# A hybrid encoder trunk in exact float32: FFN products in another order, two first weight blocks loaded together, small vectors through POOL's queue

## The chip, the cores and the metric

The kernel runs on one core of a Trainium2 chip. A core has five engines with queues of their own: TensorE (PE; its weight loads are listed as PEld), VectorE (DVE), ScalarE (ACT), GpSimd (POOL) and SyncE (SP), which here issues most of the DMA transfers. Each engine works its queue in order and waits on semaphores. The metric is device time in microseconds (us), the median of several runs.

## The reference

Two layers. Each projects x (512 x 1024) with one wide matrix, runs three mixers on the parts (retention with four heads, chunked attention with a relative bias, differential attention), gates and sums them, projects the sum, and applies a layer norm; then a SwiGLU feed-forward network (FFN) and a second norm.

```python
for l in range(DEPTH):
    h = jnp.einsum('bsd,de->bse', x, w_in[l])
    rq, rk, rv, rg, cq, ck, cv, dq, dk, dv, gates = jnp.split(h, splits, axis=-1)
    o_a = _retention(rq, rk, rv, rg, ret_norm_g[l])          # heads reshaped, left out here
    o_b = _chunk_attention(cq, ck, cv, ca_rel_bias[l])
    o_c = _diff_attention(dq, dk, dv, lam, lambda_init, da_norm_g[l])
    g = jax.nn.sigmoid(gates + b_merge[l]).reshape(B, S, N_BRANCHES, D)
    merged = sum over the branches of g[:, :, i] * (o_i @ w_branch_i[l])
    x = _layer_norm(DEEPNORM_ALPHA * x + merged @ w_out[l], ln1_g[l], ln1_b[l])
    u_gate, u_up = jnp.split(x @ w_ffn_in[l], 2, axis=-1)
    ffn = (jax.nn.silu(u_gate) * u_up) @ w_ffn_out[l]
    x = _layer_norm(DEEPNORM_ALPHA * x + ffn, ln2_g[l], ln2_b[l])
```

## The kernel before

**Numbers.** Every float32 operand is carried as a pair, hi and lo, in the type that TensorE takes at full rate. ACT casts hi, DVE subtracts to get lo (a "split"), and each product is three matmuls (`mm3`: hi by hi, hi by lo, lo by hi).

**Weights.** Weights come in blocks of up to 1 MB. A block is loaded by SP into one of four staging tiles (`st`), then split by ACT (`wh`) and DVE (`wl`) into one of three hi/lo buffer pairs. `Wt` does this in two halves (L151, L152), `Staged` in one piece (L260, L261).

**Seven products instead of eight.** Large products are done by a scheme of Strassen's kind on 2 x 2 blocks: seven products m1, m2, y, v, g, x, h, each of 24 matmuls of 512 columns, and sums of weights and activations beside them. In a `Chain` unit the weight sums are made in place, one after another, in a staging tile: the block is split for one product, then POOL issues an accumulating load (`more`, L179) that adds the next piece of weight from memory, and the result is the block of the next product of the chain: m1, then y, then x, then h. `ahead_c` makes the separate sum for g. In a `Close` unit DVE adds staged blocks (L234, L240). The activation sums are made by `Quarters.sums` (L293 to L296, then splits); the steps `s_q` (mixer) and `s_x1` (FFN) call it. `u_two` turns the seven results into outputs: x alone leads to 14 DVE operations (L740 to L746 and the callbacks); m1, g, v and y are copied out of PSUM by ACT (L734). In the FFN the callbacks are `gate_half` and `gated` (L1218), which multiply the two halves of a hidden tile (the `nat` tiles). `s_turn(pb, hf)` transposes two finished `nat` tiles on PE (L1230); `s_ready` and `s_twins` split the transposed tiles for the products of the output matrix.

**Order.** The program is a list of items, each with its weight blocks, a function and groups of side steps; weights are fetched until three blocks stand ready. Between the column tiles of an item (`between`), one group of side steps is placed; what is left follows the item.

```python
while at <= i or (at < len(items) and sum(map(len, ready)) < AHEAD):
    fetch()
pending.extend(groups)
fn(*ready.pop(0))
while pending:
    between()
```

The order of the items is written by hand. The order of the instructions on an engine's queue is then set by a scheduler, which by its own model of time lets a ready instruction pass one that waits; `keep_in_program_order` pins an instruction behind the one traced before it on its engine. So SP issues a load as soon as a staging tile is free by that model.

**The start.** The first item, `u_first`, needs three blocks: retention's q and k columns for two heads, and a gate. Block 0 is loaded in four pieces with two of the eight x tiles behind each (`load_x`), and split the same way (`split_x`, L589 and L590); the first two column tiles of block 0 run as the pieces arrive, blocks 1 and 2 follow. Retention's q and k go through `rotary` (two ACT copies, three DVE operations, then a split). After block 1 comes `vectors`: 7 loads of `rows`, a transpose on PE (`pcol`, L626), ACT's and DVE's copies of it, and 4 broadcast loads of `lv`; in layer 0 also `negate_bias`, a load, a negation and a store of the bias rows (`nrel`). All of these go through SP's queue.

**Retention.** `s_dh(h)` loads a decay tile (`dh`, 256 KB), `s_r1(h)` computes the scores (`psr`), multiplies by the decay (L795) and splits the result.

**FFN.** `u_ffn(i)` does 48 matmuls of 512 columns and its gate (`ffn_done`); `u_ffn_first` does the first two tiles by halves of the rows. `s_natural(t)` finishes the natural-layout rows of the norm (four DVE operations and two stores). Units p and q are the input products, o and w the output products; `fout_rest` does the remaining rows, and ends in `chase`, where each tile of rows is normalised behind its matmuls.

Of the kernel before, what the change touches and what calls it, by code (L numbers as in the profile page):

```python
# [17 lines left out]
P = 128  # L18
# [3 lines left out]
KT = D // P  # L22
# [4 lines left out]
DA_HEADS, DA_DH = 4, 64  # L27
# [29 lines left out]
def trunk(ctx, tc, x_in, xT_in, w_in, ret_norm_g, da_norm_g, lq1, lk1, lq2, lk2, w_a, w_b, w_c, b_merge, w_out,  # L57
# [22 lines left out]
    def f(ap):  # L80
        return ap.bitcast(F32)
# [44 lines left out]
    class Wt:  # L126


        def __init__(self, pieces, nk, beside=None):
            ncol = sum(ap.shape[1] for ap in pieces)  # L130
            n = nk * ncol
            st = wst.tile([P, 2048], F32, tag="st", name="st")[:, :n].rearrange("p (k c) -> p k c", k=nk)
            hi = wsp.tile([P, 2048], F32R, tag="wh", name="wh")[:, :n]
            lo = wsp.tile([P, 2048], F32R, tag="wl", name="wl")[:, :n]
            self.hi = hi.rearrange("p (k c) -> p k c", k=nk)
            self.lo = lo.rearrange("p (k c) -> p k c", k=nk)
            self.nk = nk
            h = max(nk // 2, 1) if beside is None else 2
            c0 = 0
            for ap in pieces:  # L140
                w = ap.shape[1]
                src = ap.rearrange("(k p) c -> p k c", p=P)
                for k in range(0, nk, nk if beside is None else h):
                    e = nk if beside is None else k + h
                    nc.sync.dma_start(st[:, k:e, c0:c0 + w], src[:, k:e])
                    if beside is not None:
                        beside[0](k, e)
                c0 += w
            for a in range(0, nk, h):
                b = min(a + h, nk)  # L150
                done = [nc.scalar.copy(self.hi[:, a:b], st[:, a:b]),  # L151
                        nc.vector.tensor_sub(self.lo[:, a:b], st[:, a:b], f(self.hi[:, a:b]))]  # L152
                if beside is not None:
                    for ins in done:
                        tc.keep_in_program_order(ins)
                    beside[1](a, b)

    class Halves:

# [395 lines left out]
    def run_items():  # L555
        ready, at = [], 0

        def fetch():
            nonlocal at
            specs, at = items[at][0], at + 1  # L560
            ready.append([])
            for sp in specs:
                first = at == 1 and not ready[-1]
                ready[-1].append(sp() if callable(sp) else Wt(*sp, beside=(load_x, split_x) if first else None))
# [12 lines left out]
        nc.tensor.transpose(warm[:, :P], ident, ident)  # L577


    def load_x(k0, k1):  # L580
        for k in range(k0, k1):
            xfs[0][k] = g(name="xf")
            nc.sync.dma_start(xfs[0][k], xT_in[P * k:P * k + P])

    def split_x(k0, k1):
        for k in range(k0, k1):
            xTs[0][k] = Pair("xT")
            src, pr = xfs[0][k], xTs[0][k]
            tc.keep_in_program_order(nc.scalar.copy(pr.hi, src))  # L589
            tc.keep_in_program_order(nc.vector.tensor_sub(pr.lo, src, f(pr.hi)))  # L590

    xTs = [[None] * KT for _ in range(DEPTH + 1)]
    xfs = [{} for _ in range(DEPTH + 1)]
# [2 lines left out]
    def layer(l):  # L596
# [8 lines left out]

        def negate_bias():
            t = small.tile([P, 96], F32, tag="nrel", name="nrel", bufs=1)
            nc.sync.dma_start(t, rel.rearrange("l h (r c) -> (l h r) c", c=96))
            nc.vector.tensor_scalar_mul(t, t, -1.0)
            nc.sync.dma_start(nrel, t)  # L610

        def vectors():
            if l == 0:
                negate_bias()

            rows = small.tile([64, P], F32, tag="rows", name="rows", bufs=1)
            nc.gpsimd.memset(rows, 0.0)
            r0 = 0
            for name, ap in (("bm", b_merge), ("rg", ret_norm_g), ("dg", da_norm_g), ("g1", ln1_g), ("b1", ln1_b),
                             ("g2", ln2_g), ("b2", ln2_b)):  # L620
                n = ap.shape[1] // P
                nc.sync.dma_start(rows[r0:r0 + n], ap[l:l + 1].rearrange("o (r c) -> (o r) c", c=P))
                v[name] = slice(r0, r0 + n)
                r0 += n
            psc = bank("pcol")
            nc.tensor.transpose(psc[:, :64], rows, ident[:64, :64])  # L626
# [49 lines left out]
        def u_first():  # L676
# [8 lines left out]

            def whole(*wts):
                ret_tables()
                banks = [bank("pt") for _ in range(2)]
                for k in range(KT):
                    for j in range(2):  # L690
                        a, c = xT[k], slice(P * j, P * j + P)
                        mm3(banks[j], wts[0].hi[:, k, c], wts[0].lo[:, k, c], a.hi, a.lo, k == 0, k == KT - 1)
                for i, w in enumerate(wts):
                    for j in range(2):
# [25 lines left out]
        def u_two(hv, acts, left_done, right_done):  # L720
# [16 lines left out]
            def x(j, ps):  # L737
                u, y, c = g(name="tu"), t["y", j], t.pop(("v", j))
                t["u", j] = u
                nc.vector.tensor_sub(u, ps, t.pop(("m1", j)))  # L740
                nc.vector.tensor_add(y, y, u)
                nc.vector.tensor_add(c, c, y)
                right_done(j, c)
                c = t.pop(("g", j))
                nc.vector.tensor_add(y, y, c)
                nc.vector.tensor_add(u, u, c)  # L746
                right_done(2 + j, t.pop(("y", j)))

            def m2(j, ps):
                c = g(name="tm")  # L750
# [5 lines left out]
                nc.vector.tensor_sub(u, ps, u)  # L756
                left_done(2 + j, u)

            use = {"x": x, "m2": m2, "h": h}
# [342 lines left out]

        w, p, q = u_two(Close(W, 0, 4, (CV, DV)), xq, v_away(cv, 64), v_away(dv, 128)), u_rvg(0), u_rvg(1)
        for (specs, fn), *groups in [
            (u_first(), [w["c"]]), (u_gate(0, 1), [w["a"], s_q(0)], [s_q(1)]), (w["m1"], [], [s_q(2)]), (u_gate(0, 2), [s_q(3)]),
            (w["g"],), (w["v"],), (w["m2"], [lam]), (w["y"], [p["c"]]), (w["x"],), (u_gate(0, 3),), (w["h"], [p["a"], s_dh(0)]),
            (p["m1"], [], [s_r1(0)]), (p["g"], [s_dh(1)]), (p["v"], [], [s_r1(1)]), (p["m2"],),
            (p["y"], [q["c"]]), (p["x"],), (u_rqk(rq, RQ, 1), [q["a"]]), (p["h"],),
            (q["m1"], [], [s_r2(0)]), (u_rqk(rk, RK, 1), [s_r2(1)], [s_r3(0)]), (q["g"], [], [s_r3(1)]),
            (q["v"], [s_dh(2)]), (q["m2"], [], [s_r1(2)]), (q["y"], [s_dh(3)]), (q["x"],), (u_cqk(0), [], [s_r1(3)]), (q["h"],),  # L1110
# [272 lines left out]

        p, q, o, w = u_fin(0), u_fin(1), fout_items(0), fout_items(1)
        for (specs, fn), *groups in [
            (u_ffn_first([8, 9]), [s_natural(0)], [s_x1(0)]),
            (p["m1"], [s_x1(1)], [p["c"], s_natural(1)]), (p["m2"], [s_x1(2)], [s_natural(2)]),
            (u_ffn(10), [s_x1(3), s_natural(3)]), (p["y"],), (p["v"],), (p["g"],), (p["x"],),
            (u_ffn(11), [], [s_turn(0, 0)]), (p["h"],), (q["m1"], [q["c"]], [s_turn(0, 1)]), (q["m2"],), (u_ffn(12),),
            (q["y"],), (q["v"],), (q["g"],), (q["x"],), (u_ffn(13), [], [s_turn(1, 0)]), (q["h"], [s_ready(0)], [s_ready(1)]),  # L1390
            (o["m1"], [], [s_turn(1, 1)]), (u_ffn(14), [s_twins(0)], [s_twins(1), o["c"]]), (o["m2"],), (o["y"],), (u_ffn(15),),
            (o["v"],), (o["x"],), (u_ffn(16),), (o["g"], [], [s_hid(0)]), (o["h"], [], [s_hid(1)]), (u_ffn(17), [s_hid(2)], [s_hid(3)]),
            (w["m1"],), (u_ffn(18), [], [w["c"]]), (w["m2"],), (w["y"],), (u_ffn(19),),
            (w["v"],), (w["x"],), (u_ffn(20),), (w["g"],), (w["h"],), (u_ffn(21),),
        ]:
            item(specs, fn, *groups)
        for it in fout_rest(0) + fout_rest(1):
# [60 lines left out]
```

## Time and profile before

| what | value |
|---|---|
| median of 3 runs | 1912.64 us (1911.21 to 1913.13) |
| the profiled execution, its own time | 1909.92 us |
| its span, first to last instruction | 1908.2 us |
| granted TensorE clock, mean | 0.997 |
| busy: PE, PEld | 1884.3 us, 1585.9 us |
| busy: DVE, ACT, POOL | 1354.5 us, 951.1 us, 101.6 us |
| DMA | 285.12 MB, 149 GB/s mean |

How to read the rows: a row of the timeline is the start in us, the duration, the engine, the line of the kernel, the operation, output tile <- input tiles, their shapes, and a count; in brackets the idle time of the engine just before, and what ended it. The table of waits gives, for an engine's line and what released it, the total, the number of times and the longest. PE's matmuls are pipelined: a row's duration is the time through the array, and the distance of two starts is the pace. "SPq" and "POOLq" are the issuing queues.

### The profile page before, as it was taken

To read this page: it belongs to the slowest core of one execution; us is meant where nothing else is said; L and a number is where in the kernel's file an instruction comes from. 1 tells how busy PE (TensorE), PEld (TensorE's weight loads), DVE (VectorE), ACT (ScalarE), POOL (GpSimd) and SP (SyncE) were. 2 spreads that over 40 slices of the span, in tenths; PEclk is the share of its full clock that TensorE was granted. 3 is DMA by queue.
4 is the path that set the end of the run, shared out by engine and by line. 5 is a ranking of instruction groups with operands and counts; after the bars stand their busy time and mean duration, and the time that the engine had idled before them with its cause. 6 is when DMAs were issued, how large, how long until landed. Compare 5 with 4: busy or idle time off the path is not lost. (4 is left out here: it accounts for less than half of the span.)

```text
span 1908.2 us, 24157 instructions
## 1 busy us (share of the span) xinstructions
PE 1884.3 (99%) x9170; PEld 1585.9 (83%) x9170; DVE 1354.5 (71%) x2157; ACT 951.1 (50%) x1581; POOL 101.6 (5%) x117
## 2 busy tenths in 40 slices
PE   9999999999999999999999999999999999999998
PEld 7888888888888878888898788888888888788886
DVE  5778866677666866886578788666775668677865
ACT  5545555566534544453255546555765344444530
POOL 0000000000001000000000000000000010010000
PEclk9999999999999999999999999999999999999999
DMA  8686343332254577664555844432322647785641
GB/s 258 189 258 164 121 163 106 118 122 67 70 193 124 165 188 188 166 159 129 153 170 175 253 131 144 165 106 94 122 78 72 215 89 189 173 215 151 157 130 44
DMA packets 240185, 285.12 MB, mean 149 GB/s; under 512 B 9550, under 2 KB 148932, under 8 KB 240068
## 3 DMA queue, kind: packets, MB, share of 16 engines
q1 hardware_dynamic: 216836, 237.43, 37.8%
q0 software_dynamic: 23232, 46.14, 13.9%
q8 instruction: 72, 1.18, 0.2%
q14 instruction: 45, 0.37, 0.1%
HBM read 260.42 MB, written 23.12 MB: 149 GB/s over the span
## 5 line engine op out<-in xcount | busy, mean ns | idle before, releaser
L122 PE MATMUL pt<-xTh,wh 128*128 128x512 f32 (+1 forms) x1328 | 497.1, 375 | 1.2 <-ACT xTh L589 1.2
L123 PE MATMUL pt<-xTl,wh 128*128 128x512 f32 (+1 forms) x1328 | 493.8, 372 | 2.8 <-DVE xTl L112 1.9
L124 PE MATMUL pt<-xTh,wl 128*128 128x512 f32 (+1 forms) x1328 | 493.7, 372 | 0.0
L151 ACT CAST wh<-st 128x1024 fp32r<-128x1024 f32 (+1 forms) x234 | 220.1, 969 | 216.9 <-PE pt L123 109.7
L152 DVE TENSOR_TENSOR wl<-st,wh 128x1024 fp32r<-128x1024 f32 (+1 forms) x234 | 257.1, 1119 | 87.3 <-ACT wh L151 81.4
L261 DVE TENSOR_TENSOR wl<-st,wh 128x2048 fp32r<-128x2048 f32 x98 | 224.2, 2288 | 118.0 <-ACT wh L260 116.4
L123 PEld LDWEIGHTS pt<-xTl,wh 128*128 128x128 f32 x1328 | 250.6, 189 | 46.0 <-DVE xTl L112 2.3
L122 PEld LDWEIGHTS pt<-xTh,wh 128*128 128x128 f32 x1328 | 250.2, 189 | 43.6 <-ACT xTh L589 1.9
L124 PEld LDWEIGHTS pt<-xTh,wl 128*128 128x128 f32 x1328 | 250.2, 188 | 43.5
L260 ACT CAST wh<-st 128x2048 fp32r<-128x2048 f32 x98 | 187.3, 1913 | 142.1 <-PE pf L124 58.1
L122 PE MATMUL pf<-wh,xTh 128*128 128x512 f32 x240 | 94.7, 395 | 0.6 <-ACT tg L734 0.6
L124 PE MATMUL pf<-wh,xTl 128*128 128x512 f32 x240 | 94.2, 392 | 0.0
L123 PE MATMUL pf<-wl,xTh 128*128 128x512 f32 x240 | 94.1, 392 | 0.0
L122 PE MATMUL pf<-wh,s43h 128*128 128x512 f32 x192 | 75.2, 391 | 0.0
L123 PE MATMUL pf<-wl,s43h 128*128 128x512 f32 x192 | 74.8, 389 | 0.0
L123 PE MATMUL pf<-wl,s12h 128*128 128x512 f32 x192 | 74.7, 389 | 0.0
L122 PE MATMUL pf<-wh,s12h 128*128 128x512 f32 x192 | 74.7, 389 | 0.0
L124 PE MATMUL pf<-wh,s12l 128*128 128x512 f32 x192 | 74.4, 389 | 0.0
L124 PE MATMUL pf<-wh,s43l 128*128 128x512 f32 x192 | 74.2, 390 | 0.0
L383 ACT COPY sw<-pt 32x512 f32<-32x512 f32 (+1 forms) x96 | 55.7, 580 | 26.9 <-PE pt L124 25.6
L1188 DVE TENSOR_TENSOR fth<-fth,pt 128x512 f32<-128x512 f32 x28 | 19.2, 685 | 51.0 <-PE pt L124 50.7
L122 PEld LDWEIGHTS pf<-wh,xTh 128*128 128x128 f32 x240 | 45.5, 190 | 10.2 <-ACT tg L734 1.0
(351 smaller groups left out, 3565.9 us busy)
## 6 DMA issues: line engine op xcount, KB each, us to landing
st<-in_w_in SPq DMA_DIRECT2D x61, 1024.0 KB, 8.2
st<-in_w_ffn_in SPq DMA_DIRECT2D x56, 512.0 KB, 5.1
st<-in_w_ffn_out SPq DMA_DIRECT2D x20, 1024.0 KB, 4.9
st<-in_w_in SPq DMA_DIRECT2D x32, 512.0 KB, 5.2
st<-in_w_ffn_in SPq DMA_DIRECT2D x16, 1024.0 KB, 8.2
st<-in_w_ffn_in POOLq DMA_DIRECT2D x16, 1024.0 KB, 9.2
st<-in_w_ffn_out POOLq DMA_DIRECT2D x16, 1024.0 KB, 8.8
st<-in_w_in POOLq DMA_DIRECT2D x12, 1024.0 KB, 11.2
```

The costliest lines, as they stand in the source:

```text
L122: nc.tensor.matmul(ps, lh, rh, start=start, stop=False)
L123: nc.tensor.matmul(ps, lh, rl, start=False, stop=False)
L124: nc.tensor.matmul(ps, ll, rh, start=False, stop=stop)
L151: done = [nc.scalar.copy(self.hi[:, a:b], st[:, a:b]), nc.vector.tensor_sub(self.lo[:, a:b], st[:, a:b], f(self.hi[:, a:b]))]
L152: nc.vector.tensor_sub(self.lo[:, a:b], st[:, a:b], f(self.hi[:, a:b]))]
L260: nc.scalar.copy(self.hi, st)
L261: nc.vector.tensor_sub(self.lo, st, f(self.hi))
L383: nc.scalar.copy(sw[half * b:half * b + half], ps[half * o:half * o + half])
L1188: nc.vector.tensor_mul(t, t, pu)
```

## The change

1. `Wt` can put off its loads and splits (`later`), and `first_blocks` loads the first two blocks in pieces, alternately, each piece with one x tile; the third block follows whole. All their splits are pinned in this order. `u_first` in layer 0 runs the matmuls of both blocks for a k before the next k.
2. `vectors` and `negate_bias` issue their loads from POOL's queue instead of SP's, with the zeroing of `rows` and the loads of `lv` pinned; in layer 0 `vectors` comes before the third block's matmuls, and `negate_bias` moves to `lam`.
3. In the mixer, `w["c"]` and `w["a"]`, `s_dh(0)`, `s_dh(1)`, `s_r1(0)` and `s_r1(1)` are placed later, by about an item.
4. In the FFN, `u_ffn(10)` moves ahead of p's m1, and every later `u_ffn` item comes one earlier; the order inside p and q is now m1, FFN, y, m2, v, x, FFN, g, h. Where g comes after x (in the FFN's p and q), its two results are added straight from PSUM (`last_right`) instead of being copied by ACT first. The side steps are placed anew.

```diff
     class Wt:
-        def __init__(self, pieces, nk, beside=None):
+        def __init__(self, pieces, nk, later=False):
...
+            if later:
+                return
+            self.load(0, nk)
+            h = max(nk // 2, 1)
+            for a in range(0, nk, h):
+                self.split(a, min(a + h, nk))
...
+    def first_blocks(*specs):
+        wts = [Wt(*sp, later=True) for sp in specs]
+        for k in range(0, KT, 2):
+            for i, wt in enumerate(wts[:2]):
+                wt.load(k, k + 2)
+                xfs[0][k + i] = g(name="xf")
+                nc.sync.dma_start(xfs[0][k + i], xT_in[P * (k + i):P * (k + i) + P])
+        wts[2].load(0, KT)
+        for k in range(0, KT, 2):
+            for i, wt in enumerate(wts[:2]):
+                src, pr = xfs[0][k + i], Pair("xT")
+                xTs[0][k + i] = pr
+                for ins in wt.split(k, k + 2):
+                    tc.keep_in_program_order(ins)
+                tc.keep_in_program_order(nc.scalar.copy(pr.hi, src))
+                tc.keep_in_program_order(nc.vector.tensor_sub(pr.lo, src, f(pr.hi)))
+        for k in range(0, KT, KT // 2):
+            for ins in wts[2].split(k, k + KT // 2):
+                tc.keep_in_program_order(ins)
+        return wts
...
         def negate_bias():
-            nc.sync.dma_start(t, rel.rearrange("l h (r c) -> (l h r) c", c=96))
+            nc.gpsimd.dma_start(t, rel.rearrange("l h (r c) -> (l h r) c", c=96))
             nc.vector.tensor_scalar_mul(t, t, -1.0)
-            nc.sync.dma_start(nrel, t)
+            nc.gpsimd.dma_start(nrel, t)
         def vectors():
-            if l == 0:
-                negate_bias()
-            nc.gpsimd.memset(rows, 0.0)
+            tc.keep_in_program_order(nc.gpsimd.memset(rows, 0.0))
...
-                nc.sync.dma_start(rows[r0:r0 + n], ap[l:l + 1].rearrange("o (r c) -> (o r) c", c=P))
+                nc.gpsimd.dma_start(rows[r0:r0 + n], ap[l:l + 1].rearrange("o (r c) -> (o r) c", c=P))
...
-                nc.sync.dma_start(lv[:, j], vec[l:l + 1].to_broadcast([P, DA_DH]))
+                tc.keep_in_program_order(nc.gpsimd.dma_start(lv[:, j], vec[l:l + 1].to_broadcast([P, DA_DH])))
         def lam():
+            if l == 0:
+                negate_bias()
...
             def whole(*wts):
-                banks = [bank("pt") for _ in range(2)]
+                banks = [[bank("pt") for _ in range(2)] for _ in range(2)]
                 for k in range(KT):
+                    for w, b in zip(wts, banks):
                         ...
                 for i, w in enumerate(wts):
+                    if i == 2:
+                        vectors()
                     for j in range(2):
-                        done(i, j, proj_T(xT, w, P * j) if i else banks[j])
-                    if i == 1:
-                        vectors()
+                        done(i, j, proj_T(xT, w, P * j) if i == 2 else banks[i][j])
...
                 right_done(j, c)
-                c = t.pop(("g", j))
+                if ("g", j) in t:
+                    last_right(j, t.pop(("g", j)))
+            def last_right(j, c):
+                y, u = t.pop(("y", j)), t["u", j]
                 nc.vector.tensor_add(y, y, c)
                 nc.vector.tensor_add(u, u, c)
-                right_done(2 + j, t.pop(("y", j)))
+                right_done(2 + j, y)
+            def gg(j, ps):
+                (last_right if ("u", j) in t else copy("g"))(j, ps)
...
-            (u_first(), [w["c"]]), (u_gate(0, 1), [w["a"], s_q(0)], [s_q(1)]), (w["m1"], [], [s_q(2)]), (u_gate(0, 2), [s_q(3)]),
-            ... (u_gate(0, 3),), (w["h"], [p["a"], s_dh(0)]),
-            (p["m1"], [], [s_r1(0)]), (p["g"], [s_dh(1)]), (p["v"], [], [s_r1(1)]), (p["m2"],),
+            (u_first(),), (u_gate(0, 1), [s_q(0)], [s_q(1), w["c"]]), (w["m1"], [], [s_q(2), w["a"]]), (u_gate(0, 2), [s_q(3)]),
+            ... (u_gate(0, 3),), (w["h"], [p["a"]]),
+            (p["m1"], [s_dh(0)]), (p["g"], [], [s_r1(0)]), (p["v"], [s_dh(1)]), (p["m2"], [], [s_r1(1)]),
...
-            (u_ffn_first([8, 9]), [s_natural(0)], [s_x1(0)]),
-            (p["m1"], [s_x1(1)], [p["c"], s_natural(1)]), (p["m2"], [s_x1(2)], [s_natural(2)]),
-            (u_ffn(10), [s_x1(3), s_natural(3)]), (p["y"],), (p["v"],), (p["g"],), (p["x"],),
-            (u_ffn(11), [], [s_turn(0, 0)]), (p["h"],), (q["m1"], [q["c"]], [s_turn(0, 1)]), (q["m2"],), (u_ffn(12),),
-            (q["y"],), (q["v"],), (q["g"],), (q["x"],), (u_ffn(13), [], [s_turn(1, 0)]), (q["h"], [s_ready(0)], [s_ready(1)]),
+            (u_ffn_first([8, 9]), [s_natural(0)], [s_x1(0)]), (u_ffn(10), [s_x1(1), s_x1(2)], [s_x1(3), s_natural(1)]),
+            (p["m1"], [s_natural(2)], [p["c"], s_natural(3)]), (u_ffn(11),), (p["y"],), (p["m2"],),
+            (p["v"],), (p["x"],), (u_ffn(12), [], [s_turn(0, 0)]), (p["g"],), (p["h"],),
+            (q["m1"], [], [q["c"]]), (u_ffn(13), [s_turn(0, 1)]), (q["y"],), (q["m2"],),
+            (q["v"],), (q["x"],), (u_ffn(14), [], [s_turn(1, 0)]), (q["g"],), (q["h"], [s_ready(0)], [s_ready(1)]),
...
-            (w["v"],), (w["x"],), (u_ffn(20),), (w["g"],), (w["h"],), (u_ffn(21),),
+            (w["v"],), (w["x"],), (u_ffn(21),), (w["g"],), (w["h"],),
```

Between the last two pairs of lines o and w keep their order; only the numbers of the `u_ffn` items there rise by one.

More of the change, by code (lines that the diff above doesn't have):

```diff
@@ L136, in __init__, with load, split @@
             self.lo = lo.rearrange("p (k c) -> p k c", k=nk)
-            self.nk = nk
-            h = max(nk // 2, 1) if beside is None else 2
+            self.nk, self.st, self.pieces = nk, st, pieces
+            if later:
[4 more added lines that the diff above has]
+                self.split(a, min(a + h, nk))
+        def load(self, a, b):
             c0 = 0
-            for ap in pieces:
+            for ap in self.pieces:
                 w = ap.shape[1]
[L142 to L147, printed above, removed]
-                c0 += w
[L149 to L156, printed above, removed]
+                nc.sync.dma_start(self.st[:, a:b, c0:c0 + w], ap.rearrange("(k p) c -> p k c", p=P)[:, a:b])
+                c0 += w
+        def split(self, a, b):
+            return [nc.scalar.copy(self.hi[:, a:b], self.st[:, a:b]),
+                    nc.vector.tensor_sub(self.lo[:, a:b], self.st[:, a:b], f(self.hi[:, a:b]))]
     class Halves:
@@ L561, in fetch @@
             ready.append([])
+            if at == 1:
+                ready[-1] += first_blocks(*specs)
+                return
             for sp in specs:
-                first = at == 1 and not ready[-1]
-                ready[-1].append(sp() if callable(sp) else Wt(*sp, beside=(load_x, split_x) if first else None))
+                ready[-1].append(sp() if callable(sp) else Wt(*sp))
         for i, (specs, fn, groups) in enumerate(items):
@@ L577, in trunk @@
         nc.tensor.transpose(warm[:, :P], ident, ident)
[L580 to L590, printed above, removed]
+    def first_blocks(*specs):
[18 more added lines that the diff above has]
+        return wts
     xTs = [[None] * KT for _ in range(DEPTH + 1)]
@@ L687, in whole @@
                 ret_tables()
-                banks = [bank("pt") for _ in range(2)]
+                banks = [[bank("pt") for _ in range(2)] for _ in range(2)]
                 for k in range(KT):
-                    for j in range(2):
[L691 to L694, printed above, removed]
-                        done(i, j, proj_T(xT, w, P * j) if i else banks[j])
-                    if i == 1:
-                        vectors()
+                    for w, b in zip(wts, banks):
+                        for j in range(2):
+                            a, c = xT[k], slice(P * j, P * j + P)
+                            mm3(b[j], w.hi[:, k, c], w.lo[:, k, c], a.hi, a.lo, k == 0, k == KT - 1)
+                for i, w in enumerate(wts):
+                    if i == 2:
+                        vectors()
+                    for j in range(2):
+                        done(i, j, proj_T(xT, w, P * j) if i == 2 else banks[i][j])
             def halves(*wts):
@@ L757, in h @@
                 left_done(2 + j, u)
-            use = {"x": x, "m2": m2, "h": h}
+            use = {"x": x, "m2": m2, "g": gg, "h": h}
             return {"c": hv.ahead_c, "a": getattr(hv, "ahead_a", None),
@@ L1104, in layer @@
         for (specs, fn), *groups in [
-            (u_first(), [w["c"]]), (u_gate(0, 1), [w["a"], s_q(0)], [s_q(1)]), (w["m1"], [], [s_q(2)]), (u_gate(0, 2), [s_q(3)]),
-            (w["g"],), (w["v"],), (w["m2"], [lam]), (w["y"], [p["c"]]), (w["x"],), (u_gate(0, 3),), (w["h"], [p["a"], s_dh(0)]),
-            (p["m1"], [], [s_r1(0)]), (p["g"], [s_dh(1)]), (p["v"], [], [s_r1(1)]), (p["m2"],),
+            (u_first(),), (u_gate(0, 1), [s_q(0)], [s_q(1), w["c"]]), (w["m1"], [], [s_q(2), w["a"]]), (u_gate(0, 2), [s_q(3)]),
+            (w["g"],), (w["v"],), (w["m2"], [lam]), (w["y"], [p["c"]]), (w["x"],), (u_gate(0, 3),), (w["h"], [p["a"]]),
+            (p["m1"], [s_dh(0)]), (p["g"], [], [s_r1(0)]), (p["v"], [s_dh(1)]), (p["m2"], [], [s_r1(1)]),
             (p["y"], [q["c"]]), (p["x"],), (u_rqk(rq, RQ, 1), [q["a"]]), (p["h"],),
```

6 lines of the change are left out of this document (3 added, 3 removed).

## The prediction

> **What bounds the kernel now.** I read the page first (busy shares), then the waits of PE, then the stretch of time around each wait on the engine that the wait names.
>
> ```profile
> PE 1884.3 (99%) x9170; PEld 1585.9 (83%) x9170; DVE 1354.5 (71%) x2157; ACT 951.1 (50%) x1581; POOL 101.6 (5%) x117
> ```
> ```profile
> core 0 of [0], span 1908.2 us
> engine line waited for: us in total, times, longest us
> PE ph L1230 <- DVE tv L1218: 6.9, 2, 3.5
> PE pt L123 <- DVE xTl L112: 1.9, 2, 1.0
> PE psr L122 <- DVE rtmp L795: 1.9, 2, 1.5
> PE warm L577 <- POOL ident masks.py:199: 1.5, 1, 1.5
> PE pt L122 <- ACT xTh L589: 1.2, 1, 1.2
> PE pt L123 <- DVE xTl L590: 0.8, 1, 0.8
> PE pf L122 <- ACT tg L734: 0.6, 2, 0.3
> ```
> PE is the bound: it is idle for 23.9 us (1908.2 - 1884.3). The edit neither adds nor removes a matmul, so all it can win is idle time of PE, and all it can lose is new idle time. The waits add up to 14.8 us; the rest is the tail of VectorE after the last matmul, which no edit touches. Three groups belong to code that changes: the start (L589, L590), the `psr` banks of `s_r1` with the `tg` rows right behind them, and `s_turn` (L1230), once in each layer.
>
> **Part 1, first two blocks together.** Before, only block 0 was interleaved with x, and ACT's cast of block 1 stood ahead of the cast of the last x tile:
>
> ```profile
> 7.59 0.39 PE L122 MATMUL pt<-xTh,wh 128*128 128x512 f32 x1
> 7.82 0.39 PE L123 MATMUL pt<-xTl,wh 128*128 128x512 f32 x1
> ```
> ```profile
> 15.81 1.05 ACT L151 CAST wh<-st 128x1024 fp32r<-128x1024 f32 x1 [3.10 <-DMA st<-in_w_in]
> ```
> ```profile
> 15.80 0.39 PE L124 MATMUL pt<-xTh,wl 128*128 128x512 f32 x1
> 17.42 0.50 PE L122 MATMUL pt<-xTh,wh 128*128 128x512 f32 x1 [1.24 <-ACT xTh L589]
> 18.76 0.50 PE L123 MATMUL pt<-xTl,wh 128*128 128x512 f32 x1 [0.84 <-DVE xTl L590]
> ```
> A 512-column matmul starts every 0.23 us (7.59 to 7.82), so the two gaps cost 1.39 + 1.11 = 2.5 us (17.42 - 15.80 and 18.76 - 17.42, less 0.23 each). Now a step of k has 12 matmuls (2.7 us) instead of 6 (1.4 us), for one more 128 KB of weights. What is late next: x and two blocks are the bytes that x, block 0 and block 1 were, so the last x tile lands about when block 1 landed, 15.8 us, and is split by some 17; PE, at 0.23 us each from 7.6 us, comes to k = 6 after 66 more matmuls, at 23 us. Nothing is late, and the 2.5 us go; the pinned order of the splits also takes away what put block 1's cast first. The price: the four rotaries of blocks 0 and 1 come due together, at about 28 us (90 matmuls after 7.6), where two of them were begun by 22.
>
> ```profile
> 22.23 0.68 DVE L385 TENSOR_TENSOR rot<-pt,cosr 128x512 f32<-128x512 f32 x1
> ```
> ```profile
> 20.50:42.20 21.70, 21.70 (x96) 17.66 (x95) 15.49 (x21) 12.12 (x18) 1.67 (x2) 1.00 0.72 214
> 42.20:69.50 27.30, 27.30 (x123) 22.59 (x122) 20.01 (x29) 12.65 (x16) 1.28 (x1) 1.00 0.90 272
> ```
> A rotary with its split is four such operations, so 4 x 4 x 0.68 = 11 us of DVE from 28 to 39 us, under the third block (48 x 0.23 = 11 us). In the two windows (stretch, length, busy PE, PEld, DVE) DVE had 35.5 us to do from 20.5 to 69.5 us; it now has some 38 for it, from 28 to 66. The cover is thin: at worst the subtracts of `u_gate(0, 1)`, as much as one block (2.3 us, part 4), wait behind all rotaries, and PE waits as long. I take 2.5 us won; ends 3.2 (the small gaps before 12 us too) and 0.2.
>
> **Part 2, small vectors through POOL.** SP loses 11 transfers per layer and the two of `nrel`:
>
> ```profile
> 9.30 3.43 SPq L608 DMA_DIRECT2D nrel<-in_rel  x1
> ...
> 24.91 0.43 SPq L175 DMA_DIRECT2D st<-in_w_in  x1
> ```
> ```profile
> L626 PE MATMUL pcol<-ident,rows x2: 271/274/276, 31.0 to 971.1; 64*128 64x64 f32 x2
> ```
> ```profile
> 959.03 0.55 POOL L494 TENSOR_TENSOR rs<-rs,mhalf 128x1 f32<-128x1 f32 x1 [9.24 <-DVE rs L493]
> 994.17 1.31 POOL L179 DMA_DIRECT2D st<-in_w_in  x1 [34.59 <-DVE rot L387]
> ```
> ```profile
> st<-in_w_ffn_in SPq DMA_DIRECT2D x16, 1024.0 KB, 8.2
> st<-in_w_ffn_in POOLq DMA_DIRECT2D x16, 1024.0 KB, 9.2
> st<-in_w_ffn_out POOLq DMA_DIRECT2D x16, 1024.0 KB, 8.8
> st<-in_w_in POOLq DMA_DIRECT2D x12, 1024.0 KB, 11.2
> ```
> The first weight load after `nrel` and the vectors left SP at 24.91; PE never waited for it, so sending it sooner is worth 0. On POOL, 7 `rows` and 4 `lv` transfers now stand ahead of the accumulating loads; at the 1.31 us that a 1 MB one takes there they are 14 us. In layer 0 they start near 1 us and `rows` is wanted at 28: cost 0. In layer 1 they are now pinned behind the last `rs`, 959.6 us: 7 x 1.31 puts the last issue at 968.8, and the transpose stood at 971.1 on PE. With a landing of under 2.3 us that costs nothing, with the 8.8 us of a 1 MB accumulating load 6.5 us. The 512-byte rows move at most 12 KB, so they lie near the small end: I take 0. `negate_bias` in `lam` costs 0: only the later bias tables read `nrel`.
>
> A rule speaks against this part: the Trainium skill, "DMA: Bandwidth & Descriptors", section "Issuing engine by pattern", gives simple loads to Sync and calls that path generally faster than GpSimd's. The rows agree in sign (8.2 against 9.2 us for the same 1 MB, though POOL's accumulates). By the fit on the same page, 2.0 us plus bytes over 436e3, an estimate puts the landing at 970.8 and the cost at 0 as well.
>
> **Part 3, mixer, one tile later.** `s_dh(0)`, `s_r1(0)` and `s_r1(1)` move by one item, with the same DMA on SP, 30 matmuls, 4 multiplies and 3 splits for each head.
>
> ```profile
> DVE rtmp L795 <- DMA dh<-in_decay: 4.9, 1, 4.9
> ```
> ```profile
> 1083.36 0.63 PE L123 MATMUL pf<-wl,xTh 128*128 128x512 f32 x1
> 1083.78 0.63 PE L124 MATMUL pf<-wh,xTl 128*128 128x512 f32 x1
> ```
> At the first `s_r1` of a layer DVE stands 4.9 us for `dh`; the backlog reaches PE at the second. The price is 1.9 + 0.6 us of waits, and after the wait of layer 1 some seven matmuls 0.42 us apart instead of 0.23 (1.4 us): 3.9 us. The way from `s_dh(0)` to `s_r1(0)` stays a block and a half, 8 us, but SP is freer: layer 1's vectors no longer sit among these loads. Against it, the second `s_r1` now meets the additions of m2 instead of the copies of v. Ends: all 3.9 won, or as much lost again; I take half, 1.9 us won.
>
> **Part 4, FFN order.** The wait at the first `s_turn` of layer 0; layer 1 repeats it.
>
> ```profile
> 662.80 1.28 POOL L179 DMA_DIRECT2D st<-in_w_ffn_in  x1 [24.50 <-DMA saved<-z]
> ```
> ```profile
> 672.60 3.73 ACT L260 CAST wh<-st 128x2048 fp32r<-128x2048 f32 x2 [7.30 <-DMA st<-in_w_ffn_in]
> ```
> ```profile
> 674.55 2.29 DVE L261 TENSOR_TENSOR wl<-st,wh 128x2048 fp32r<-128x2048 f32 x1 [4.97 <-ACT wh L260]
> ...
> 677.36 0.68 DVE L745 TENSOR_TENSOR ty<-ty,tg 128x512 f32<-128x512 f32 x1
> ```
> ```profile
> 685.56 0.39 PE L123 MATMUL pf<-wl,xTh 128*128 128x512 f32 x1
> 685.79 0.40 PE L124 MATMUL pf<-wh,xTl 128*128 128x512 f32 x1
> ```
> Read backwards: PE wants `tv` (L1218); DVE was blocked 4.97 us by ACT's cast of block h; ACT stood 7.30 us for h's sum, which left POOL at 662.80 and came 9.8 us later. Between x and h was one FFN item (48 x 0.23 = 11 us of PE); now there are that item and g (16.4 us), and h's hi/lo buffers come free from x instead of g, 5.4 us later, so the cast comes into line about when the sum has landed. Second, g after x: of x's 14 DVE operations (0.68 us each) 6 go to g's item, three of them from ahead of the awaited `tv` (this L745 and both L746: 2.0 us), and four ACT copies per layer vanish. m2 moves behind y; its additions are wanted by x, 11 us later. From y's start to `s_turn` PE has four blocks and an FFN item, 33 us; DVE has six splits (14), m2 (2.8), x (5.5), an FFN item's gate (1.4) and about 8 of left-over `natural` and `s_x1` work: 32, the last splits behind `s_turn`. Both waits go: 6.9 us won; ends 0 and 6.9. What is late next: g's six additions now fall beside h and `s_ready`: 4.1 + 4.1 + 2.8 + two splits (4.6) = 15.6 us of DVE in 11 us of PE, with the FFN item ahead as reserve. For this I add 1.0 us (ends 0 and 3). y and x keep their 11 us. One `hid` tile more is alive, and `u_ffn(21)` moves ahead of the last blocks: 0, since the output blocks that read it are hidden work of the same order.
>
> A rule here: the Trainium skill, "TensorE: Matmul & The Clock Gate", Part 1, says that some 3.4 us of idleness bring the clock to half. The rows differ: half pace follows a wait of at most 1.5 us in part 3, and after this wait of 3.4 us matmuls are 0.23 us apart (685.56 to 685.79). By the rule the 1.4 us of part 3 would not hang on its wait, and the sum would be 0.7 us smaller.
>
> **Sum.** -2.5 + 0 - 1.9 - 6.9 + 1.0 = -10.3 us. The profiled execution took 1909.92 us (its span and 1.7 around it): 1899.6. The median of the runs, 1912.64, is 2.7 higher, so the forecast is 1902.3, rounded to 1902.
>
> **Rivals.**
> *The sum stays late* (0.14): h's cast waits as before and only the moved additions help, 2.0 us per layer: -2.5 - 1.9 - 4.0 + 1.0, so 1905. For it: 9.8 us for the sum, and y's copies that already run late.
> *No gain from the order* (0.10): DVE's amount of work is the limit, the waits move to the next `s_turn` or to o's m1, and part 3 gives nothing; only the start is won: 1910. Against it: DVE is idle for 4.97 us right there.
> *`rows` late* (0.10): 6.5 us on PE at layer 1's transpose: 1909. For it stands 8.8 us as the shortest landing from POOL in section 6, against it the size.
> *Slower* (0.08): the chained sum of w. `w["c"]` now stands behind the tanh stores of the second item. If SP keeps that order, the load leaves at 50 us; + 8.2 + 11.2 + a split of 4.2 it is there at 73.6, where PE wants g at 66.4: 7.2 us per layer, 1917. It decides from 5.2 us per layer on. Against it: before, SP sent this load at 24.91, ahead of every such store:
>
> ```profile
> 43.43 0.46 SPq L1047 DMA_DIRECT2D th<-th  x1
> ```
> **How the numbers follow.** The forecast has 0.58. Its own range is 1898 to 1905: part 3 whole or nothing, up to 3 us of new waits. The full range, 1897.5 to 1909.5, takes in the late sum and the late `rows`, and leaves out the slower case and the one at 1910. A change under 0.2% (3.8 us) can't be told from none here: faster is 0.58 + 0.14 + half of the `rows` case = 0.77, same 0.15, slower 0.08.
>
> **What would show it.** Right: no L589 or L590 row and no L1230 row in PE's waits; ACT's wait for `st<-in_w_ffn_in` in the p unit gone; `tg` copies down by eight. Wrong: a PE wait at `pcol`, or for a split of `u_gate(0, 1)` near 39 us, longer waits at `psr`, or o's m1 waiting for `s_ready`.

## The result, and the profile after

The changed kernel takes 1894.86 us (median of six runs, 1893.49 to 1896.34) against 1912.34 us for the kernel before (six runs): ratio 0.991, 95% interval 0.9898 to 0.9923. The gain is 17.5 us where the forecast's sum had 10.3, and the time lies below the forecast range. The profiled execution took 1896.34 us, span 1894.5 us.

Busy shares on the page of the changed kernel:

```profile
PE 1881.4 (99%) x9170; PEld 1584.9 (84%) x9170; DVE 1355.1 (72%) x2159; ACT 946.2 (50%) x1575; POOL 113.9 (6%) x141
```
PE has the same 9170 instructions and is still the bound; it is idle for 13.1 us (1894.5 - 1881.4) instead of 23.9. Its table of waits after (line, releaser: total us, times, longest):

```profile
core 0 of [0], span 1894.5 us
engine line waited for: us in total, times, longest us
PE pt L122 <- ACT wh L154: 2.0, 1, 2.0
PE warm L578 <- POOL ident masks.py:199: 1.5, 1, 1.5
PE px L504 <- DVE z L495: 0.6, 2, 0.3
PE pt L122 <- ACT xTh L596: 0.2, 1, 0.2
```
The `ph`, `psr`, `tg` and `xTl` rows are gone. New are a wait of 2.0 us at the start and two of 0.3 us at the norm's transposes. At the first turn PE runs straight through (timeline of PE after):

```profile
683.83 0.39 PE L124 MATMUL pt<-xTh,wl 128*128 128x512 f32 x1
684.06 1.03 PE L1249 MATMUL ph<-ident,tv 128*128 128x128 f32 x8
684.85 0.48 PE L122 MATMUL pf<-wh,s43h 128*128 128x512 f32 x1
```
What feeds it changed as the diff says. ACT's copies of g fell from 20 to 12 (groups by tile, before and then after; the last one is now in the mixer, at 1140.8 us):

```profile
L734 ACT COPY tg<-pf x20: 579/589/622, 77.8 to 1679.1; 128x512 f32<-128x512 f32 x20
```
```profile
L746 ACT COPY tg<-pf x12: 579/588/610, 77.5 to 1140.8; 128x512 f32<-128x512 f32 x12
```
And DVE hardly waits for the decay tile any more (DVE's waits, before and then after):

```profile
DVE rtmp L795 <- DMA dh<-in_decay: 10.0, 2, 5.0
```
```profile
DVE rtmp L814 <- DMA dh<-in_decay: 0.2, 1, 0.2
```

PE has the same matmuls per stage in both kernels, so stages can be laid side by side by the starts of the same transposes on PE: `pcol`, the first `psc` of the chunked attention, the first `px` of the norm. In us, from the traces:

| stage | before | before, second profile | after | after, second profile |
|---|---|---|---|---|
| start to `pcol`, layer 0 | 31.0 | 33.5 | 30.8 | 30.3 |
| `pcol` to `psc`, layer 0 | 234.2 | 234.7 | 232.9 | 232.9 |
| `px` of layer 0 to `pcol` of layer 1 (FFN) | 383.4 | 385.5 | 379.0 | 379.0 |
| `pcol` to `psc`, layer 1 | 243.2 | 243.0 | 239.6 | 239.6 |
| `px` of layer 1 to PE's end (FFN) | 362.5 | 365.2 | 358.5 | 358.5 |

The rest of the mixer, `psc` to `px`, takes 322.5 us in both layers of all four.

Between the two profiled executions named in the forecast that is -0.2 at the start, -4.9 in the mixers, -8.3 in the FFNs and -0.3 behind PE's end: 13.6 us, which is 1909.92 - 1896.34. The other 3.9 us of the 17.5 are not in this pair: the profile before was 2.4 us faster than the median of its runs, the profile after 1.5 us slower than that of its own. Why the second column is so much longer than the first is the main finding below.

### The profile page after: what moved, and what is told of

Read it like the earlier page. It is cut to its first block, busy times and chain, and to the rows that moved or that the text cites. A ratio compares the mean times of both kernels' runs of the same rounds, so it can differ in the third digit from the quotient of the medians.

```text
span 1894.5 us, 24166 instructions
## 1 busy us (share of the span) xinstructions
PE 1881.4 (99%) x9170; PEld 1584.9 (84%) x9170; DVE 1355.1 (72%) x2159; ACT 946.2 (50%) x1575; POOL 113.9 (6%) x141
## 5 line engine op out<-in xcount | busy, mean ns | idle before, releaser
L122 PE MATMUL pt<-xTh,wh 128*128 128x512 f32 (+1 forms) x1328 | 497.2, 375 | 2.3 <-ACT wh L154 2.0
L122 PEld LDWEIGHTS pt<-xTh,wh 128*128 128x128 f32 x1328 | 250.1, 189 | 44.3 <-ACT wh L154 2.5
L122 PE MATMUL pf<-wh,xTh 128*128 128x512 f32 x240 | 93.4, 389 | 0.0
L122 PE MATMUL pf<-wh,s43h 128*128 128x512 f32 x192 | 75.5, 393 | 0.1
L122 PE MATMUL pf<-wh,s12h 128*128 128x512 f32 x192 | 74.9, 390 | 0.0
L124 PEld LDWEIGHTS pf<-wh,xTl 128*128 128x128 f32 x240 | 45.1, 188 | 9.4
```

The costliest lines, as they stand in the source:

```text
L122: nc.tensor.matmul(ps, lh, rh, start=start, stop=False)
L124: nc.tensor.matmul(ps, ll, rh, start=False, stop=stop)
```

## The experiments

Theory A: each part wins the waits of PE in its own stage as the profile shows them. Theory B: the psr waits go because SP is freed of the small vectors. Theory C: a long wait of PE is paid twice, by itself and by matmuls at half pace behind it (0.43 us from one start to the next instead of 0.23), which the one profiled execution of the kernel before happened not to show at the turns. All kernels of a group ran on one chip, with runs of the kernel before among them; the groups ran on three different chips.

### The four parts, each alone

Each kernel is the kernel before with one of the four numbered parts of the diff; there is no other edit. The kernel before: 1911.74 us, 27 runs.

> The kernel before with the change of the first two blocks alone (vectors and the orders as before). In the changed kernel PE's transpose of the small vectors stands at 30.84 us instead of 31.04, so the new wait of 2.0 us for the cast of block 1's first piece, with half-pace matmuls until 10.9 us, ate the 2.5 us that went. Theory A (each part wins exactly the PE waits of its own stage): -0.2 us, no more than 1 us either way, PE again waits about 2 us near 5.3 us for ACT's cast of a weight piece. Rival (the new wait comes from POOL's small transfers, which slow the first loads: the third transfer landed at 7.08 instead of 6.20): with the vectors on SP behind the blocks the third transfer lands at 6.2, the wait is 1.2 us and the time falls by 1 to 2.5 us.

> The kernel before with the small vectors on POOL's queue alone. Theory A: nothing on PE's path waits for them, 0 within 1 us; the waits at psr (1.9 us) and for the dh tile (4.9 us on DVE) stay. Rival B (the psr waits went because SP is free of layer 1's vectors): the dh loads leave SP earlier, the psr and tg waits and the half-pace stretch vanish, -4.9 us.

> The kernel before with the mixer's steps (w's sums, the decay loads, the first two score steps) one item later alone. Theory A: the psr and tg waits vanish by the shift itself, -4.9 us in the profiled execution (index by index the two traces differ by 1.3 us there in layer 0 and 3.6 us in layer 1). Rival B (SP's relief did it): psr waits stay at 1.5 us or more, 0 to -1 us.

> The kernel before with the new FFN order and g added from PSUM alone. Theory A: both waits at the transposes of s_turn go (7.2 us) and the waits in the first FFN item shrink (1.3 us): -8.5 us in the profiled execution. Rival C (waits of 3.5 us also cost half-pace stretches that the one profiled execution of the kernel before happened not to show): the median falls by 10 to 12 us, more than the waits of the profile.

| part alone | us | difference | ratio, 95% interval |
|---|---|---|---|
| 1, start | 1910.27 | -1.5 | 0.999 (0.9981 to 0.9999) |
| 2, small vectors through POOL | 1914.20 | +2.5 | 1.0015 (1.0006 to 1.0023) |
| 3, mixer | 1909.64 | -2.1 | 0.9988 (0.9979 to 0.9996) |
| 4, FFN order | 1900.19 | -11.5 | 0.9938 (0.9924 to 0.9952) |

The FFN order carries two thirds of the gain, and more than Theory A gives it: the two turn waits and the two `xTl` waits of the kernel before are 6.9 and 1.9 us, less 0.6 us for two new `px` waits, and the interval of the gain begins at 9.2. (In a second profile of the kernel before, below, the turn waits are 7.7 us, so this alone is a narrow margin.) The mixer's shift removes the psr waits without any help from part 2; here are all of PE's waits in that kernel:

```profile
PE ph L1230 <- DVE tv L1218: 6.9, 2, 3.8
PE pt L123 <- DVE xTl L112: 1.9, 2, 1.0
PE warm L577 <- POOL ident masks.py:199: 1.5, 1, 1.5
PE pt L122 <- ACT xTh L589: 1.3, 1, 1.3
PE pt L123 <- DVE xTl L590: 1.1, 2, 0.8
```
With part 2 alone `psr L122 <- DVE rtmp L795` stays, once, at 1.7 us, and the layer-1 mixer stage stays at 243.4 us (with part 3 alone 239.4). Theory B falls for layer 1. In layer 0 the runs decide nothing: part 2 alone takes 232.9 us there and part 3 alone 233.0, and six profiles with neither part spread from 233.1 to 234.7. In its profile part 3 wins the 5.0 us that Theory A gives it in its own two stages; the medians show 2.1 (0.8 to 4.0). One thing that can make the difference is that layer 1's stage isn't always as long as the first profile has it: with part 1 alone it takes 241.7 us, without any half pace in it.

Part 2 alone loses at the start, which neither expectation had; in the timeline of PE and the groups by tile:

```profile
19.94 0.50 PE L122 MATMUL pt<-xTh,wh 128*128 128x512 f32 x1 [2.77 <-ACT xTh L589]
```
```profile
L624 PE MATMUL pcol<-ident,rows x2: 272/272/273, 35.0 to 974.9; 64*128 64x64 f32 x2
```
The last (eighth) x tile comes late: ACT casts it at 19.27 us, where seven profiles with the old start and SP's vectors have 16.4 to 18.1. Six matmuls at half pace follow, and `pcol` stands at 35.0 us, where those seven have 30.7 to 34.0. The four differences add up to -12.6 us, 4.9 short of the whole change; that is little more than the intervals together allow.

### The half pace behind the turn

First the kernel before, unchanged, profiled a second time.

> The kernel before, unchanged, in a second profiled execution: the first had the two turn waits of 3.4 and 3.5 us and hardly a slow matmul behind them. Theory C: this one shows five to fifteen matmuls at 0.43 us behind at least one of the turns, a lower mean clock, and a span of 1910 us or more. If it shows none, the half pace is rarer than the times say.

It took 1917.56 us, at the upper end of fifteen other executions on its chip (1912.10 to 1917.95); mean granted clock:

```profile
core 0: 1915.8 us, clock 0.994
```
Its page has the same 9170 matmuls, and they are busy for 5.5 us longer than in the first profile (1884.3 us). So most of the 7.6 us between the two spans is slower work of PE, not waiting:

```profile
PE 1889.8 (99%) x9170; PEld 1590.1 (83%) x9170; DVE 1355.1 (71%) x2157; ACT 950.9 (50%) x1581; POOL 101.4 (5%) x117
```
The forecast read the first turn from the execution with clock 0.997 and found 0.23 us between matmuls behind it. Here is the same place in this one (timeline of PE):

```profile
688.23 1.44 PE L1230 MATMUL ph<-ident,tv 128*128 128x128 f32 x7 [4.08 <-DVE tv L1218]
689.32 0.78 PE L122 MATMUL pf<-wh,xTh 128*128 128x512 f32 x1
689.89 0.63 PE L123 MATMUL pf<-wl,xTh 128*128 128x512 f32 x1
690.32 0.63 PE L124 MATMUL pf<-wh,xTl 128*128 128x512 f32 x1
...
692.03 0.40 PE L122 MATMUL pf<-wh,xTh 128*128 128x512 f32 x1
692.26 0.40 PE L123 MATMUL pf<-wl,xTh 128*128 128x512 f32 x1
```
Five matmuls from 689.89 to 692.03 start 0.43 us apart instead of 0.23 (1.0 us lost), and the transposes and the first matmul ahead of them lose another 0.6. At the second turn nine such matmuls follow a wait of 3.6 us, and at the start six follow the wait for the last x tile. The same stretches stand behind the turns in the profiles of part 1 alone (eight matmuls at each), of part 2 alone (three and none) and of part 3 alone (four and ten). The first profile of the kernel before, with none at either, was the exception. The FFN stage of layer 0 (`px` to `pcol`) follows the count of slow matmuls at its turn: 383.4 us with none, 384.4 with three, 385.2 with four, 385.5 with five, 386.3 with eight.

What they cost in the time of the whole kernel is asked by keeping PE busy in the wait:

```diff
                     ps = bank("ph")
+                    if (pb, hf, fp) == (0, 0, 0):
+                        for _ in range(28):
+                            tc.keep_in_program_order(nc.tensor.transpose(ps[:, :P], ident, ident))
```

> The kernel before with 28 extra transposes of the identity put on TensorE right ahead of the first transposes of each layer's s_turn(0, 0); they write the ph bank that the true ones then overwrite, and no other instruction changes its place. At 0.106 us each (7 of the ph transposes took 684.50 to 685.24 us) they take about 3.0 us, which lies inside the wait of 3.4 to 3.8 us, so the transposes behind them start when they did. Theory C (an idle TensorE of about 3.4 us is paid twice, by the wait and by some nine matmuls at 0.43 us instead of 0.23 us behind it, in most executions though not in the profiled one of the kernel before): with TensorE kept busy the slow matmuls go, 1.5 to 2.5 us for each layer: 1908 to 1909 us against 1911.7, and no matmul at 0.43 us in the profile behind either turn. Theory A (the price of a wait is the wait): no change, 1911.5 to 1912.5 us, with 0 to 0.4 us lost where the transposes outlast the wait.

> As turn_filled, with 12 transposes in place of 28: 1.3 us of work inside a wait of 3.4 to 3.8 us, so TensorE still stands idle for 2.0 to 2.6 us before the turn. With 28 the kernel became 5.0 us faster and no matmul behind a turn ran at half pace. If what calls the half pace is the length of one idle stretch, and 2 us is short enough, the same gain, 1907 to 1909 us. If any idle stretch of 2 us calls it as well, no gain, 1911.5 to 1913 us with matmuls at 0.43 us behind the turns. Something between means that it depends on the execution.

With 28 transposes 1907.74 us against 1912.69: ratio 0.9977 (0.9968 to 0.9985), 5.0 us faster (2.9 to 6.1). PE in its profile:

```profile
681.75 2.57 PE L1229 MATMUL ph<-ident 128*128 128x128 f32 x22
684.15 0.27 PE L1233 MATMUL ph<-ident,tv 128*128 128x128 f32 x1
685.04 0.98 PE L1233 MATMUL ph<-ident,tv 128*128 128x128 f32 x7 [0.61 <-DVE tv L1218]
685.78 0.47 PE L122 MATMUL pf<-wh,xTh 128*128 128x512 f32 x1
686.09 0.39 PE L123 MATMUL pf<-wl,xTh 128*128 128x512 f32 x1
686.32 0.39 PE L124 MATMUL pf<-wh,xTl 128*128 128x512 f32 x1
```
The first row holds 22 of the 28; they begin at 681.10. From there to 685.04 us only one useful transpose is done, as before, and yet the kernel is faster: full pace follows at once, at the second turn too. The FFN stage of layer 0 takes 383.5 us, as in the profile without slow matmuls. That is Theory C, and Theory A (no change) falls. The two stretches of the second profile of before come to some 3.8 us (1.6 and 2.2), inside the interval; whether the turns account for all of the 5.0 us isn't shown, since the half pace in layer 1's retention is missing from this one profile as well.

With 12 transposes it is 1910.93 us against 1913.44: 0.9984 (0.9975 to 0.9993). The two intervals overlap, so whether 12 do less than 28 stays open. Its profile holds both outcomes: behind 2.19 us of idleness at the first turn and 2.40 us at the second full pace follows, and behind 1.43 us and 0.31 us in layer 1's retention half pace:

```profile
685.67 0.98 PE L1233 MATMUL ph<-ident,tv 128*128 128x128 f32 x7 [2.19 <-DVE tv L1218]
686.40 0.47 PE L122 MATMUL pf<-wh,xTh 128*128 128x512 f32 x1
686.72 0.39 PE L123 MATMUL pf<-wl,xTh 128*128 128x512 f32 x1
...
1081.97 0.38 PE L122 MATMUL psr<-rqkh 128*128 128x256 f32 x1 [1.43 <-DVE rtmp L795]
...
1082.89 0.50 PE L122 MATMUL pf<-wh,xTh 128*128 128x512 f32 x1 [0.31 <-ACT tg L734]
...
1084.02 0.63 PE L123 MATMUL pf<-wl,xTh 128*128 128x512 f32 x1
1084.45 0.63 PE L124 MATMUL pf<-wh,xTl 128*128 128x512 f32 x1
```

### Parts together

Parts 3 and 4; then parts 1, 3 and 4, which is the changed kernel without POOL's queue.

> Parts 3 and 4 of the change together, without the new start and without POOL's queue. If the parts add up, 2.1 + 11.5 = 13.6 us faster than before, 1898 us. If the mixer's shift is worth more where the FFN's waits are gone (the FFN change alone still showed psr 1.5 us, tg 0.6 us and a stretch of half pace in layer 1's mixer), about 11.5 + 3.6 = 15.1 us, 1896.5 us. If instead the gain beyond the sum of the parts sits with the start or with POOL's queue, no more than 13.6 us.

> The changed kernel without part 2: the small vectors are loaded through SP's queue as before, where they were. Part 2 alone cost 2.5 us, all of it at the start (the seventh x tile came late). If that cost is there in the changed kernel too, this is 1 to 2.5 us faster than the changed kernel, 1892.5 to 1894 us; if the new order of the start hides it (the profile of the changed kernel shows no wait for an x tile behind the first two), the same within 1 us, 1894 to 1896 us; if SP's queue needs the relief once the other parts are in, slower, 1896.5 to 1898 us.

Parts 3 and 4 give 1898.13 us, 0.9924 (0.991 to 0.9937): 14.6 us faster, a middle value between the two expectations. Part 3 is worth 3.0 us there against 2.1 alone, a difference smaller than the intervals. Adding part 1 gives 1893.92, 0.9902 (0.9888 to 0.9915), 4.2 us more, where part 1 alone gave 1.5. So of the 4.9 us beyond the sum of the parts, by the medians, 1.0 comes with part 3 (14.6 against 13.6), 2.7 with part 1 and the rest with part 2, which costs 1.3 in company (18.8 against 17.5) instead of 2.5. This is a division of medians from different chips, each with an interval of 2 to 5 us, and no more than that. A part of it is scatter of the start, where seven profiles of one and the same order differ by 3.3 us at `pcol`.

Without part 2 the first loads come sooner. ACT's casts of block 1's first piece and of the last x tile, in the changed kernel and then in the one without part 2 (timeline of ACT):

```profile
7.10 0.62 ACT L154 CAST wh<-st 128x512 fp32r<-128x512 f32 x1 [2.15 <-DMA st<-in_w_in]
...
19.16 0.62 ACT L596 CAST xTh<-xf 128x512 fp32r<-128x512 f32 x1
```
```profile
5.90 0.62 ACT L154 CAST wh<-st 128x512 fp32r<-128x512 f32 x1 [0.93 <-DMA st<-in_w_in]
...
15.34 0.62 ACT L596 CAST xTh<-xf 128x512 fp32r<-128x512 f32 x1
```
POOL issues eleven small transfers from 1.5 us on. A second profile of the changed kernel has these casts at 6.43 and 18.38 us, and part 1 alone, with the vectors on SP's queue, at 6.26 and 16.27. So the last x tile comes 2 to 4 us later with POOL's transfers beside it; for block 1's first piece the second pair of profiles differs by 0.2 us only, so nothing is shown. `pcol` stands at 30.8 against 28.1 us here, but at 30.4 with part 1 alone, so the queue by itself doesn't set it. In the whole kernel's time the two can't be told apart (0.991 and 0.9902, with intervals that overlap).

### The wait of the new start

In the changed kernel PE's queue has the first product of block 1 ahead of the lo products of block 0 (timeline of PE after; the row at 5.01 is two matmuls):

```profile
5.01 0.73 PE L122 MATMUL pt<-xTh,wh 128*128 128x512 f32 x2 [0.24 <-ACT xTh L596]
7.77 0.80 PE L122 MATMUL pt<-xTh,wh 128*128 128x512 f32 x1 [2.03 <-ACT wh L154]
8.36 0.63 PE L123 MATMUL pt<-xTl,wh 128*128 128x512 f32 x1
8.79 0.63 PE L124 MATMUL pt<-xTh,wl 128*128 128x512 f32 x1
```
PE stands for 2.03 us; block 0's four lo products for the first x tile are at hand from 5.7 us on (DVE ends `xTl` then). Six matmuls at half pace follow. The next kernel loads and splits both x tiles ahead of block 1, in each of the four rounds:

```diff
-            for i, wt in enumerate(wts[:2]):
-                wt.load(k, k + 2)
+            wts[0].load(k, k + 2)
+            for i in range(2):
                 xfs[0][k + i] = g(name="xf")
                 nc.sync.dma_start(xfs[0][k + i], xT_in[P * (k + i):P * (k + i) + P])
+            wts[1].load(k, k + 2)
```
The splits are reordered alike.

> The changed kernel with another order of the first loads and of their splits: two k of block 0, both x tiles, then two k of block 1, in place of block 0, x tile, block 1, x tile. TensorE's own order then has block 0's twelve products for the first two x tiles ahead of the first of block 1, so that it should have work while block 1's first piece lands (7.1 us). If the 2.03 us wait for block 1's first cast, and the eleven matmuls at 0.43 us around it, are what ate the gain of the new start, pcol comes at 28.5 to 29.5 us instead of 30.84 and the time is 1892.5 to 1893.5 us. If the loads themselves set the end of this stage (the last x tile lands near 19 us), or another wait takes its place, pcol stays within 0.5 us and the time within 0.5 us of the changed kernel, 1894.5 to 1895.5 us.

1894.09 us, 0.9903 (0.9889 to 0.9916). The wait is gone (a gap of 0.09 us is left, at 7.79), and `pcol` comes at 28.7 us, as the first reading said; the time is 0.8 us below that of the changed kernel on another chip, less than that reading had. Last the changed kernel again, and one with both mends, on one chip:

> The changed kernel once more, on the chip of the next kernel, so that part 2 and the order of the first loads are compared against it directly: 0.991 of the time before, 1894 to 1897 us, TensorE's one long wait again that for block 1's first cast at about 2 us.

> The changed kernel with both mends: both x tiles ahead of block 1 (x1_first) and the small vectors back on SP's queue (no_pool). Each alone was about 1 us faster than the changed kernel had been on another chip. If they mend two things (TensorE's wait for block 1, the small transfers that delay the first blocks), 1.5 to 2.5 us faster than after_again, about 1892.5 us; if both mend the one wait at 5.7 us, the same as either of them, 1 us faster than after_again, about 1894 us; if chips differ more than the kernels, no difference from after_again.

The changed kernel: 1895.38 us (1894.27 to 1895.88, four runs), 0.9903 (0.9889 to 0.9916). Its wait for block 1's first cast was 0.5 us this time, not 2, but seven matmuls at half pace were there again, and `pcol` came at 30.3. So the length of that wait isn't what sets `pcol`. Part 1 alone is alike (a wait of 0.7 us, eight matmuls at half pace, `pcol` at 30.4), while the kernel without part 2 has a wait of 0.8 us, full pace behind it and `pcol` at 28.1. In the two slow cases the pair of matmuls ahead of the wait already runs at half pace (1.22 us for both instead of 0.73), so that here the wait isn't shown to be its cause.

With both mends: 1894.10 us (1893.69 to 1894.71), 0.9898 (0.9883 to 0.9913), `pcol` at 28.7, no earlier than with either mend alone (28.7 and 28.1). The middle expectation comes nearest, but that the vectors' queue mends anything at the start is not shown. It is 1.3 us better than the changed kernel by the medians, which the intervals against the kernel before don't separate.

## Why the prediction was wrong

The waits of PE that it meant to remove went, and none of the rivals took place. What failed are the prices, and the largest miss is not in a part of the change but in the step from the profiled execution to the median. Forecast 1902.3 before rounding, measured 1894.86: 7.4 us. Of these, 4.2 lie in that step; the other 3.3 are the parts together, by the two profiles (-13.6 where -10.3 were summed).

**The sum's last term, +2.7 us (missed by 4.2).** The forecast took 1899.6 from the profiled execution and added the distance of that execution from the median, as if it were a constant of the chip. It isn't. At the turns the price of a wait was taken to be the wait alone; the runs show half pace behind the waits as well, which the profiled execution had less of than most, and which goes when the waits go. The kernel with 28 transposes shows it directly: -5.0 us with the turn as late as ever. How the 2.7 us divide is not shown: the start has its share, since the profiled execution has `pcol` at 31.0 us and the middle one of seven at 32.5. Nor is it shown why the changed kernel's median lies 1.5 us below its own profiled execution.

**Part 4's rule, read the wrong way.** The forecast set the row (0.23 us behind a 3.40 us wait) against the Trainium skill, "TensorE: Matmul & The Clock Gate", Part 1, and sided with the row. It used the page only to doubt the 1.4 us of part 3; that the page would charge the turns more, it did not ask. Four other profiled executions with the old FFN order and an unfilled turn have half pace behind at least one turn. The same section says that the activity window runs freely, so that the count of slow matmuls varies from run to run; that agrees with 0, 3, 4, 5 and 8 slow matmuls at the same turn here. Where it gives about 3.4 us of idleness as the condition, the rows differ: half pace also follows 3.03 us at a turn, and 1.43 and 0.31 us in layer 1's retention.

**Part 4, -6.9 + 1.0 (profile: -8.3; alone, by the medians, -11.5).** The two turn waits went, by the causes named: ACT's 7.30 us for h's sum is not there, and the copies fell by eight. The 1.0 us for new waits did not come: neither `s_ready` nor o's m1 waits. Not counted at all were the two `xTl L112` waits of 1.0 us at the first FFN item, which stood in the table of waits. With part 4 alone they are gone, and two `px` waits of 0.3 us each are there instead; which of the moved side steps does it was not tested.

**Part 3, -1.9 (profile: -4.9; alone, by the medians, -2.1).** Half of 3.9 was taken because the second `s_r1` now meets m2's additions. It met them without a wait, and in the profile all 3.9 us came and 1.0 more; the half had no row behind it, and that the median of part 3 alone lies near it is luck. DVE's 5.0 us for `dh` became 0.2, but not because the load came sooner: in layer 1 it leaves 93.8 us after `pcol` before and 94.4 after, and the first multiplication stands 102.5 and 102.6 us after it. So DVE now has other work in those 5 us.

**Part 1, -2.5 (profile: -0.2; alone, by the medians, -1.5).** The two gaps for the last x tile went as forecast. "Nothing is late" looked only at the last tile and at the rotaries. Late was the first piece of block 1, at 7.1 us, and PE's queue, on which the sums of both blocks are interleaved, put it ahead of work that was ready. That wait measured 0.5 to 2.0 us in four profiles; in three of them six to eight matmuls at half pace stood beside it, which the sum didn't have either.

**Part 2, 0 (alone, by the medians, +2.5).** Layer 1 was right: `rows` are issued by 957.8 us and `pcol` at 965.2 waits for nothing. An issue of such a row takes 0.50 to 0.73 us, not the 1.31 us assumed (timeline of POOL after):

```profile
957.29 0.50 POOL L631 DMA_DIRECT2D rows<-in_ln_b  x1
```
At the start the forecast asked when the vectors land, not what they delay: the last x tile, which PE waits for in the old start. With the new start no wait for it is left, and the totals with and without part 2 can't be told apart.

## What to carry to other kernels

Price a wait of PE with the half pace that may follow it, and look at more than one execution: where the profiled one is faster than the median, the difference may be a cost that its own rows don't show, and it is not to be carried over when the waits behind it go. Transposes of an identity into a bank that is about to be overwritten test this at once; inside the wait they didn't make the turn later here. A small transfer put on another queue can be paid by the large transfers beside it, as the last x tile paid here; ask what those feed. In interleaved sums, check what PE's queue has first while a second operand is still on its way.

## What the runs showed of the hardware

Half pace is not tied to the length of one wait alone: 0 slow matmuls behind 3.40 us, 5 behind 4.08, 8 behind 3.84 (part 1 alone), 3 behind 3.03 (part 2 alone), 10 behind 3.15 (part 3 alone), 0 behind 2.19, 7 behind 1.43 + 0.31. Where it came inside the kernel it began up to some 2 us after the wait had ended (1084.02 behind 1081.97), and the slow matmuls lasted some 1 to 4 us. Slow matmuls count as busy time of PE (1889.8 us against 1884.3 for the same instructions), so the table of waits doesn't show them. What decides between half and full pace behind a given wait stays open. Executions of the kernel before spread from 1912.10 us at clock 0.997 to 1917.95 at 0.993 on one chip; those of the changed kernel from 1894.27 to 1895.88 at 0.998 to 0.999.
